# Attention in pairs of heads on the two row halves of TensorE, in one written-out order

## The chip, the cores and the metric

The kernel runs on one core of a Trainium2 chip. The metric is the device time of one execution in microseconds (us). Three executions of the kernel before took 1080.45 to 1080.77 us, median 1080.64 us.

In the text PE is TensorE (matrix products), DVE is VectorE, ACT is ScalarE, POOL is GpSimd and SP is SyncE, which here issues most of the transfers. Each engine runs its own instructions strictly one after the other; they meet only through semaphores.

## The reference

A small decoder of two layers on x of 512 tokens by 1024 features, in float32. Layer 0 mixes tokens with a gated linear recurrence, layer 1 with attention over the 128 keys of each query that an indexer scores highest; a squared-ReLU MLP follows each. The part that the change is about, shortened:

```python
q, c, qi, ki, wi = split(h @ w_in)             # 16 heads x 64, latent 128, indexer 8 heads x 64
c = rms_norm(c, kv_norm_g)                     # (512, 128): keys and values come from c
q_lat = einsum('bshd,hdc->bshc', q, w_uk) * ATT_SCALE
dots = relu(einsum('bqhd,bsd->bqhs', qi, ki))  # 8 indexer heads, 64 rows deep
score = einsum('bqh,bqhs->bqs', wi, dots)      # causal, else -inf
_, idx = top_k(score, 128)
logits = einsum('bqhc,bqkc->bqhk', q_lat, c[idx]) + rel_bias[bucket(dist)]
p = softmax(logits)                            # per head, over the chosen keys
o = einsum('bqhk,bqkc->bqhc', p, c[idx]); o = einsum('bshc,hcv->bshv', o, w_uv)
x = x + o @ w_o
x = x + square(relu(norm(x) @ w_up)) @ w_down  # the MLP, twice in the program
out = rms_norm(x, final_norm_g)                # only at the very end
```

## The kernel before

**Numbers in two halves.** A value v is kept as a high part (v rounded to fp32r) and a low part (v minus the high part); a product is three PE matmuls: high by high, low by high, high by low. ACT makes the high part with a cast (`wh`, `kh`, `pth`), DVE or POOL the low part with a subtraction (`wl`, `kl`, `ptl`).

**Weights.** The program is a sequence of weight units of 128 x 1024 (`PLAN`, `SEQ`). `prep` loads a unit over SP into `raw`, ACT casts it to `wh`, DVE subtracts to `wl`; for the units named in `LO_DMA` ACT writes -raw and a POOL transfer adds the weight on top. `unit(u)` prepares the units up to `LA = WH - 1` ahead; WH is 6, so six pairs `wh`, `wl` exist. One unit of eight 128 x 128 blocks feeds 24 matmuls of 512 columns.

**Phases.** Recurrence, MLP of layer 0, attention, w_o, MLP of layer 1, output norm. The MLP's down product is a Strassen scheme in quarters (`prod`); its last eight units (`sd1`) accumulate rows of two token tiles (`t` = 0, 1), unit by unit, each unit both tiles. Then `row` forms the two last row tiles, `rstd` their norm and `store` writes them.

**Attention.** `a_idx` multiplies out the indexer's q and k. `idx_head(h)` then takes one indexer head: its q is stacked, high part in 64 of the 128 rows and low part in the other 64 (`stack`, four half-height instructions per two heads), and so is k (`kih`, `kil`), which gives for each of the query tiles t = 1, 2, 3 (256, 384, 512 keys) two full-height matmuls into `ix`. ACT applies the ReLU, DVE (five times of 24 POOL) adds it to `score[t]`. The top 128 are found by 16 rounds of 8 for each tile (`topk_round`: `MAX8`, then `MATCH_REPLACE8` on DVE; both tiles of a round are interleaved); `topk_mask` makes a 0/-1e38 mask. Tile 1 and tiles 2 and 3 in turn are done first, then the rest of 2 and 3.

Meanwhile PE forms q for two heads per unit (`ev_q`: DVE scales, ACT and POOL stack the halves), k per head (`k_head`: three 512-column matmuls on weights that hold the head twice) and values (`v_group`). For a head, `qk` forms the logits of four query tiles by two matmuls each and adds the mask by a bf16 matmul with the identity; `qk_t` adds the bias and finds the row maximum (DVE), `qk_e` takes exponentials (ACT), `norm_p` divides (POOL), `tr` transposes on PE, `tr_ev` splits the result (ACT, DVE), `pv_head` multiplies by the values and `pv_ev` splits the output.

**What sets the order.** A scheduler sorts the whole program's instructions by the order in which they are written and by when it expects operands and buffers. Attention is written as a string `ATT_HEAD` and then a loop over heads in which `ATT_LOOP` gives the order of the steps of heads i, i-2, i-4 and i-5.

Of the kernel before, what the change touches and what calls it, by code (L numbers as in the profile page):

```python
# [33 lines left out]
WH = 6  # L34
NB = 58
NWARM = 10
SCORE_POOL = {(1, 4), (1, 5), (1, 6), (2, 6), (2, 7)}
V_DVE = {(0, 1), (0, 2)}

ATT_HEAD = ("q M p3 q q F p1 p1 q L3 q L1 L2 p1 q p2 p2 L0 p2 p1 k0 k1 p2 p1 p1 q A1 A0 v00 v"
            "01 p1 v02 n0 k2 n1 v03 q p2 p1 p1000")

ATT_LOOP = "KAa0Bk1b2xyzeGnfgm"
V_ITER = 6
WO_ITER = 4
BL = 2
TL = 2
VL = 1  # L50
# [46 lines left out]
def build_plan():  # L97
# [19 lines left out]
    for l in range(2):  # L117
        if l == 1:
# [3 lines left out]
            add("uk", [("uk", [(0, j) for j in range(g * 8, g * 8 + 8)]) for g in range(2)])  # L122
            add("a_q", lin_units("w_att", range(8), range(A_Q, A_Q + 8), 0))
            add("uv", [("uv", [(0, j) for j in range(8)])])
            add("w_o", lin_units("w_o", range(8), range(8), 3))
# [26 lines left out]
LO_DMA = {PLAN[n][0] + i for n, w in (("a_idx", range(5)), ("a_c", (0,)), ("a_q", range(8)), ("uv", (0,))) for i in w}  # L152

# [3 lines left out]
def tile_trunk(ctx: ExitStack, tc: tile.TileContext, xT, wu, prm, bias, out):  # L157
# [51 lines left out]
    state = {"next": 0}  # L209
# [26 lines left out]
    def prep(u):  # L236
# [3 lines left out]
        if UK0 <= u < UK0 + 2:  # L240
# [25 lines left out]
        for c in ((slice(0, S), slice(S, 2 * S)) if u == 0 else (slice(0, 2 * S),)):  # L266
# [4 lines left out]
            if u not in LO_DMA:  # L271
                nc.vector.tensor_sub(wl[:, c], raw[:, c], wh[:, c])  # L272
# [4 lines left out]
    def prep_to(n):  # L277
        while state["next"] < min(n, NU):
            prep(state["next"])
# [10 lines left out]
    def unit(u):  # L290
        n = u + 1 + LA
# [92 lines left out]
    def rsqrt_tok(m, w=4):  # L384
        s = st(w, "sq")
        nc.scalar.sqrt(s, m)
        y = st(w, "y")
# [7 lines left out]
    def diag(y, act=False):  # L395
# [3 lines left out]
        nc.vector.tensor_sub(dl, y, yh)  # L399
        idb = ident.unsqueeze(1).to_broadcast([P, 4, P])  # L400
        res = []
        for v in (y, dl):
            dg = bt(F32R, "dg")
            if act:
                for t in range(4):
                    nc.scalar.activation(dg[:, t * P:(t + 1) * P], ident, AF.Identity, scale=v[:, t:t + 1])
                res.append(dg)
                continue
# [5 lines left out]
    def bcast(dg, name):  # L414
        ps = pt("bc")
        nc.tensor.matmul(ps, lhsT=ones_r, rhs=dg[0], start=True, stop=False)
        nc.tensor.matmul(ps, lhsT=ones_r, rhs=dg[1], start=False, stop=True)
        b = bt(F32, name)
# [285 lines left out]
    def mlp(l, nin, up_hooks, finish):  # L704
# [31 lines left out]
        def prod(name, hooks=None):  # L736

            u, units = PLAN[name]
            for i, (kind, (_, j)) in enumerate(units):
# [666 lines left out]
```

## Time and profile before

| | |
|---|---|
| Median of three executions | 1080.64 us |
| Profiled execution, its own time | 1078.22 us |
| Its span, first to last instruction | 1076.4 us |
| PE busy | 1053.7 us, 98% |
| DVE busy | 758.0 us, 70% |
| ACT busy | 632.4 us, 59% |
| POOL busy | 141.0 us, 13% |
| Mean granted PE clock | 0.997 of full |

The rows that follow come from the profiled execution, so a time of day in them counts from the start of its span. A PE record is longer than the place it takes in the stream: consecutive matmuls overlap, and what one costs is the distance to the start of the next (below: its pitch). Attention runs from about 520 us (first `ix` product) to 692.5 us (first `w_o` product).

### The profile page before, as it was taken

The page shows a single profiled execution, that of the slowest core. Times are in us where ns is not written, and L with a number is a line of the kernel's source. Part 1 is how long each engine was busy: PE and PEld are TensorE (multiplying, and loading weights), DVE is VectorE, ACT ScalarE, POOL GpSimd, SP SyncE. Part 2 cuts the span into 40 slices and gives each one's busy share as a digit, 9 for nine tenths or more (in the row PEclk, how much of TensorE's full clock was granted, in tenths as well). Part 3 has the DMA queues.
Part 4 walks back from the last instruction along what each step waited for, and adds up shares of the span by engine and source line. Part 5 has one row for each costly group of instructions (what it writes and reads, how often), then busy time and mean ns, then how long its engine had stood idle before and what let it go on. Part 6 is the DMA issues. An engine that isn't in the chain of part 4 may idle for free.

```text
span 1076.4 us, 13486 instructions
## 1 busy us (share of the span) xinstructions
PE 1053.7 (98%) x4852; PEld 867.1 (81%) x4852; DVE 758.0 (70%) x1183; ACT 632.4 (59%) x1056; POOL 141.0 (13%) x202
## 2 busy tenths in 40 slices
PE   9999999999999999999999799999999999999996
PEld 6778888888888888888787588888888888888885
DVE  8879984555555469975799979655554544568995
ACT  7589554454544456768855898544544444456473
POOL 0000031000000000006355664221000000000000
PEclk9999999999999999999999999999999999999999
DMA  8322242444444445579662411023344344444552
GB/s 292 141 78 69 89 157 98 154 140 142 135 135 137 140 144 186 181 210 274 137 155 81 143 54 40 1 98 118 106 133 144 128 155 137 157 137 152 178 199 79
DMA packets 42691, 146.16 MB, mean 136 GB/s; under 512 B 4864, under 2 KB 4864, under 8 KB 42624
## 3 DMA queue, kind: packets, MB, share of 16 engines
q1 hardware_dynamic: 40032, 136.86, 38.5%
q0 software_dynamic: 2160, 7.87, 4.0%
q8 instruction: 38, 0.62, 0.2%
q10 hardware_dynamic: 432, 0.58, 0.2%
q14 instruction: 29, 0.24, 0.1%
HBM read 143.18 MB, written 2.10 MB: 135 GB/s over the span
## 4 chain that ended last, share of the span: by engine, by line
PE 83%; DVE 8%; ACT 5%; issue 2%; POOL 1%; DMA 0%; DVEq 0%; ACTq 0%; POOLq 0%
PE mm L298 15%; PE mm L299 15%; PE mm L300 15%; PE sp L753 9%; PE sp L751 9%; PE sp L752 9%; PE o L1168 3%; DVE work L933 2%; DVE m L928 2%; PE tr L1143 1%; DVE wl L272 1%; ACT wh L270 1%; PE qk L1097 1%; PE qk L1096 1%; PE qk L1099 1%
## 5 line engine op out<-in xcount | busy, mean ns | idle before, releaser
L270 ACT CAST wh<-raw 128x1024 fp32r<-128x1024 f32 (+1 forms) x228 | 237.6, 1049 | 345.7 <-PE mm L299 217.1
L272 DVE TENSOR_TENSOR wl<-raw,wh 128x1024 fp32r<-128x1024 f32 (+1 forms) x213 | 259.3, 1222 | 209.9 <-ACT wh L270 209.4
L298 PE MATMUL mm<-xh,wh 128*128 128x512 f32 x752 | 293.0, 390 | 0.4 <-ACT xh L358 0.4
L299 PE MATMUL mm<-xl,wh 128*128 128x512 f32 x752 | 292.9, 390 | 0.0
L300 PE MATMUL mm<-xh,wl 128*128 128x512 f32 x752 | 292.8, 389 | 0.0
L299 PEld LDWEIGHTS mm<-xl,wh 128*128 128x128 f32 x752 | 141.2, 188 | 30.3 <-DVE xl L360 1.0
L298 PEld LDWEIGHTS mm<-xh,wh 128*128 128x128 f32 x752 | 141.1, 188 | 29.7 <-ACT xh L358 0.9
L300 PEld LDWEIGHTS mm<-xh,wl 128*128 128x128 f32 x752 | 141.2, 188 | 29.3
L751 PE MATMUL sp<-wh,ah 128*128 128x512 f32 x320 | 124.9, 391 | 0.0
L753 PE MATMUL sp<-wh,al 128*128 128x512 f32 x320 | 124.6, 389 | 0.0
L752 PE MATMUL sp<-wl,ah 128*128 128x512 f32 x320 | 124.5, 389 | 0.0
L751 PEld LDWEIGHTS sp<-wh,ah 128*128 128x128 f32 x320 | 60.1, 188 | 12.7 <-ACT t L714 0.5
L753 PEld LDWEIGHTS sp<-wh,al 128*128 128x128 f32 x320 | 60.1, 188 | 12.6
L752 PEld LDWEIGHTS sp<-wl,ah 128*128 128x128 f32 x320 | 60.1, 188 | 12.2
L371 POOL TENSOR_TENSOR sq<-sq,sq 128x512 f32<-128x512 f32 x21 | 33.0, 1571 | 198.9 <-ACT sq L367 173.9
L269 POOL DMA_DIRECT2D wl<-in_wu_dram x15 | 13.2, 880 | 335.1 <-ACT wl L268 326.9
L233 DVE TENSOR_TENSOR al<-h,ah 128x512 fp32r<-128x512 f32 x80 | 54.1, 685 | 1.5 <-ACT ah L231 1.4
L751 PE MATMUL sp<-wh,sh 128*128 128x512 f32 x128 | 50.1, 391 | 0.0
L752 PE MATMUL sp<-wl,sh 128*128 128x512 f32 x128 | 49.8, 389 | 0.0
L753 PE MATMUL sp<-wh,sl 128*128 128x512 f32 x128 | 49.8, 392 | 0.0
L716 ACT ACTIVATE h<-t 128x256 f32<-128x256 f32 x128 | 46.5, 410 | 2.1
L231 ACT CAST ah<-h 128x512 fp32r<-128x512 f32 x80 | 46.6, 617 | 0.5
(258 smaller groups left out, 1634.4 us busy)
## 6 DMA issues: line engine op xcount, KB each, us to landing
raw<-in_wu_dram SPq DMA_DIRECT2D x244, 512.0 KB, 3.4
wl<-in_wu_dram POOLq DMA_DIRECT2D x15, 512.0 KB, 8.0
bias<-in_bias_dram SPq DMA_DIRECT2D x16, 256.0 KB, 3.1
x<-in_xT_dram SPq DMA_DIRECT2D x8, 256.0 KB, 6.3
out_dram<-out SPq DMA_DIRECT2D x6, 256.0 KB, 2.1
raw<-in_wu_dram SPq DMA_DIRECT2D x2, 256.0 KB, 3.6
gB<-in_prm_dram SPq DMA_DIRECT2D x2, 256.0 KB, 5.4
out_dram<-out ACTq DMA_DIRECT2D x2, 256.0 KB, 2.7
```

The costliest lines, as they stand in the source:

```text
L231: nc.scalar.copy(h, src)
L233: nc.vector.tensor_sub(l, src, h)
L270: nc.scalar.copy(wh[:, c], raw[:, c])
L272: nc.vector.tensor_sub(wl[:, c], raw[:, c], wh[:, c])
L298: nc.tensor.matmul(ps, lhsT=wh, rhs=xh, start=first, stop=False)
L299: nc.tensor.matmul(ps, lhsT=wh, rhs=xl, start=False, stop=False)
L300: nc.tensor.matmul(ps, lhsT=wl, rhs=xh, start=False, stop=last)
L371: nc.gpsimd.tensor_add(self.acc, self.acc, sq)
L716: nc.scalar.square(hq[r][half][:, p * HS:(p + 1) * HS], t[:, half * HS:(half + 1) * HS])
L751: nc.tensor.matmul(ps, lhsT=ah[:, c], rhs=wh[:, n], start=first, stop=False)
L752: nc.tensor.matmul(ps, lhsT=ah[:, c], rhs=wl[:, n], start=False, stop=False)
L753: nc.tensor.matmul(ps, lhsT=al[:, c], rhs=wh[:, n], start=False, stop=last)
```

## The change

Seven edits.

1. **Row halves.** Two heads now lie one in rows 0 to 63 and one in rows 64 to 127, and each product of 64 rows is issued twice in a row, once on each half of the array (`rows3`, `tile_position`). A pair of heads takes 3 x 2 half-height matmuls where it took 2 x 2 full-height ones with stacked parts. q and k are split with full-height instructions, `stack` is gone. The k weights hold two heads beside each other: 8 `k_head`, `k_hi`, `k_lo` in place of 16, and one `uk` unit in place of two.
2. **Index scores.** ReLU is applied in PSUM for tiles 2 and 3 and DVE reads it there; tile 1 (all eight heads) goes to POOL.
3. **Engines.** Scaling q moves from DVE to ACT and POOL, all value low parts to POOL, the mask's multiplication from ACT to POOL.
4. **Top-k.** Tile 1 goes with tile 3 for eight rounds and then with tile 2 for eight, then 2 and 3.
5. **Order.** The string `ATT` of 530 steps, each of one engine, is issued word for word by `tc.manual_schedule()`. Weight units are prepared by steps `W`; the low parts of the first four `w_o` units are separate steps `Y`. Two of the eight q units come later (`a_r`).
6. **Buffers.** WH 6 to 5 (lookahead of four units, none inside `ATT`), NB 58 to 62.
7. **End.** The last three units of `sd1` are held and run token tile by token tile. The final norm of a row tile has fewer steps (`rstd1`).

```diff
-WH = 6
-NB = 58
+WH = 5
+NB = 62
...
-ATT_HEAD = ("q M p3 q q F p1 p1 q L3 q L1 L2 p1 q p2 p2 L0 p2 p1 k0 k1 p2 p1 p1 q A1 A0 v00 v"
...
-ATT_LOOP = "KAa0Bk1b2xyzeGnfgm"
...
+NQ = 6
+ATT = (
+    "M0.0 M1.0 q.0 M2.0 p.0 q.1 p.1 W.4 M3.0 M4.0 L.0 p.2 q.2 p.3 u1.1 u2.1 p.4 F0.0 p.5 p.6 F1.0 p.7 q.3 W.5  "
...
+    def rows3(pss, w, lts, rts, last):
+        for n, (lt, rt) in enumerate(((lts[0], rts[0]), (lts[1], rts[0]), (lts[0], rts[1]))):
+            for e in range(2):
+                nc.tensor.matmul(pss[e], lhsT=lt[HR[e]], rhs=rt[HR[e], :w], start=(n == 0), stop=(last and n == 2),
+                                 tile_position=(64 * e, 0))
...
+    def idx_pair(j):
+        q = qi.pop(j)
         for t in (1, 2, 3):
             w = (t + 1) * P
...
+            pss = [pt("ix")[:, :w] for _ in range(2)]
+            rows3(pss, w, [a[:, t * P:(t + 1) * P] for a in q], (kih, kil), True)
+            for e in range(2):
+                if t == 1:
...
+                    nc.gpsimd.tensor_add(score[t][:, :w], score[t][:, :w], rl)
+                    continue
+                nc.scalar.activation(pss[e], pss[e], AF.Relu)
...
-            topk_round((1, 3 - i % 2))
+            topk_round((1, 3 if i < TOPK // 16 else 2))
...
-        if qs:
-            nc.vector.tensor_mul(qf, ps, ab["r8"])
...
+    def q_scale(i):
+        nc.gpsimd.tensor_mul(qf[i], qf[i], ab["r8"])
...
-    def qk(h, part):
-        q = qs[h // 2][h % 2]
-        kh, kl = kst[h]
...
+        for t in PARTS[part]:
             w = (t + 1) * P
             n = max(256, w)
...
+            rows3(pss, n, [a[:, t * P:(t + 1) * P] for a in qs[p]], k, t == 0)
+            for h, pst in zip(heads, pss):
+                if t:
...
+                    nc.tensor.matmul(pst, lhsT=identb, rhs=mask[t][:, :n], start=False, stop=True)
...
+    with tc.manual_schedule():
+        for w in ATT.split():
+            k, i = w.split(".")
...
             for i, (kind, (_, j)) in enumerate(units):
                 w = unit(u + i)
-                wh, wl, ah, al = w if len(w) == 4 else w + aop[j].pop(kind)
+                held.append((j, w if len(w) == 4 else w + aop[j].pop(kind)))
...
+                if len(units) - 4 < i < len(units) - 1 and name == "sd1":
+                    continue
                 for t in range(2):
-                    for p in range(2):
+                    for (j, (wh, wl, ah, al)), p in ((g, p) for g in held for p in range(2)):
...
+        def rstd1(i):
+            s = st(1, "fs")
+            nc.scalar.activation(s, ss[:, i, 0:1], AF.Sqrt, scale=1.0 / D, bias=me[0][:, i:i + 1])
...
```

Of `ATT`, the letters that the text uses: q forms q, V values, K keys, p is one step of the top-k, y a mask, A, B and C are the logits of a pair for tiles 0 and 1, 2, 3, T transposes, G multiplies by the values.

PE, first index scores. Before: `qia` and `qib` are the stacked q of two heads, `kih` and `kil` k's two parts, one row a full-height matmul:

```order
L864 MATMUL ix_4414<-kih_4192,qia_4280 128x256
L865 MATMUL ix_4414<-kil_4193,qia_4280 128x256
L864 MATMUL ix_4420<-kih_4192,qia_4280 128x384
L865 MATMUL ix_4420<-kil_4193,qia_4280 128x384
L864 MATMUL ix_4426<-kih_4192,qia_4280 128x512
L865 MATMUL ix_4426<-kil_4193,qia_4280 128x512
L864 MATMUL ix_4432<-kih_4192,qib_4281 128x256
```

The same place now; `qih` and `qil` are the parts of two heads, and of two rows that differ only in the `ix` number the first works in rows 0 to 63 and the second in rows 64 to 127:

```order
L897 MATMUL ix_4398<-kih_4185,qih_4270 128x256
L897 MATMUL ix_4399<-kih_4185,qih_4270 128x256
L897 MATMUL ix_4398<-kih_4185,qil_4272 128x256
L897 MATMUL ix_4399<-kih_4185,qil_4272 128x256
L897 MATMUL ix_4398<-kil_4186,qih_4270 128x256
L897 MATMUL ix_4399<-kil_4186,qih_4270 128x256
L897 MATMUL ix_4414<-kih_4185,qih_4270 128x384
L897 MATMUL ix_4415<-kih_4185,qih_4270 128x384
```

Two heads took four matmuls per width, and now take six of half height, in three twins.

PE, logits of tiles 2 and 3 in the loop over heads. Before, one head (`qb`, its keys `kh` and `kl`), with the masks:

```order
L1096 MATMUL qk_5469<-kh_5282,qb_4797 128x384
L1097 MATMUL qk_5469<-kl_5284,qb_4797 128x384
L1099 LDWEIGHTS identb
L1099 MATMUL qk_5469<-mask_4211,identb 128x384
L1096 MATMUL qk_5474<-kh_5282,qb_4797 128x512
L1097 MATMUL qk_5474<-kl_5284,qb_4797 128x512
L1099 LDWEIGHTS identb
L1099 MATMUL qk_5474<-mask_4212,identb 128x512
```

Now tile 3 of a pair of heads (two `qk` numbers), one of the 24 such blocks in the loop:

```order
L897 MATMUL qk_5376<-kh_5267,qh_5179 128x512
L897 MATMUL qk_5377<-kh_5267,qh_5179 128x512
L897 MATMUL qk_5376<-kh_5267,ql_5188 128x512
L897 MATMUL qk_5377<-kh_5267,ql_5188 128x512
L897 MATMUL qk_5376<-kl_5274,qh_5179 128x512
L897 MATMUL qk_5377<-kl_5274,qh_5179 128x512
L1177 LDWEIGHTS identb
L1177 MATMUL qk_5376<-mask_4205,identb 128x512
L1177 LDWEIGHTS identb
L1177 MATMUL qk_5377<-mask_4205,identb 128x512
```

The mask matmuls stay full height and follow the twins directly, so the array goes from half height to full height and back at each block.

DVE, late in the top-k (tiles 2 and 3). Before, `qf` (scaled q) and `kl` stand between the searches:

```order
L928 MAX m_692_5069<-work_4614 128x8
L928 MAX m_693_5071<-work_4607 128x8
L1015 TENSOR_TENSOR qf_4984<-mm_4959,rB_545_4357 128x512
L933 MATCH_REPLACE work_4614<-m_692_5069,work_4614 128x384
L933 MATCH_REPLACE work_4607<-m_693_5071,work_4607 128x512
L928 MAX m_694_5075<-work_4614 128x8
L928 MAX m_695_5077<-work_4607 128x8
L1070 TENSOR_TENSOR kl_5045<-k_5039,kh_5043 128x512
```

Now at the same place:

```order
L964 MAX m_654_5000<-work_4817 128x8
L964 MAX m_655_5002<-work_4600 128x8
L969 MATCH_REPLACE work_4817<-m_654_5000,work_4817 128x384
L969 MATCH_REPLACE work_4600<-m_655_5002,work_4600 128x512
L964 MAX m_660_5033<-work_4817 128x8
L964 MAX m_661_5035<-work_4600 128x8
L969 MATCH_REPLACE work_4817<-m_660_5033,work_4817 128x384
L969 MATCH_REPLACE work_4600<-m_661_5035,work_4600 128x512
```

The searches follow each other; the other DVE work of attention stands behind them.

## Rows read from the trace of the kernel before

**Rows 1.** The page, part 1: busy time, share of the span, instructions.

```profile
PE 1053.7 (98%) x4852; PEld 867.1 (81%) x4852; DVE 758.0 (70%) x1183; ACT 632.4 (59%) x1056; POOL 141.0 (13%) x202
```

**Rows 2.** Stages: window, length, busy PE, PEld, DVE, ACT, POOL, clock, DMA.

```profile
520.63:540.90 20.27, 19.66 (x99) 16.70 (x98) 16.10 (x28) 14.92 (x32) 8.35 (x10) 1.00 0.44 112
540.90:580.00 39.10, 39.10 (x178) 32.45 (x178) 39.07 (x123) 22.88 (x37) 23.32 (x22) 1.00 0.63 149
580.00:616.01 36.01, 27.84 (x135) 20.86 (x134) 35.97 (x100) 25.97 (x62) 22.00 (x29) 0.95 0.30 98
616.01:652.74 36.73, 36.53 (x230) 30.66 (x229) 30.12 (x93) 33.24 (x90) 22.65 (x49) 1.00 0.20 64
652.74:669.40 16.66, 16.66 (x109) 14.18 (x109) 15.70 (x50) 14.89 (x44) 8.09 (x22) 1.00 0.11 32
```

**Rows 3.** What PE waited for, 560 to 620: us, times, longest.

```profile
PE qk L1096 <- ACT kh L1068: 4.6, 3, 2.0
PE qk L1096 <- DVE stat L1112: 2.2, 1, 2.2
```

**Rows 4.** PE in order of time, value products (o) of one head.

```profile
685.54 0.48 PE L1168 MATMUL o<-pth,vh 128*128 128x512 f32 x1
685.86 0.40 PE L1168 MATMUL o<-ptl,vh 128*128 128x512 f32 x1
686.09 0.40 PE L1168 MATMUL o<-pth,vl 128*128 128x512 f32 x1
...
686.33 0.34 PE L1168 MATMUL o<-pth,vh 128*128 128x384 f32 x1
686.51 0.34 PE L1168 MATMUL o<-ptl,vh 128*128 128x384 f32 x1
...
686.86 0.28 PE L1168 MATMUL o<-pth,vh 128*128 128x256 f32 x1
686.98 0.28 PE L1168 MATMUL o<-ptl,vh 128*128 128x256 f32 x1
```

**Rows 5.** Chain that ended last, 684 to 688: start, us, what.

```profile
684.70 1.09 PE tr L1143 x10
```

**Rows 6.** DVE busy in the searches (MAX8, MATCH_REPLACE8), q scaling, masks.

```profile
540.31:599.20 58.89, 24.52 (x48) 0.97 0.43 102
...
540.31:599.20 58.89, 27.33 (x96) 0.97 0.43 102
...
L1015 DVE TENSOR_TENSOR qf<-mm,rB 128x512 f32<-128x512 f32 x6 | 4.0, 665 | 0.0
...
L938 DVE TENSOR_TENSOR work<-work,score x3: 403/541/671, 574.3 to 598.5; 128x256 f32<-128x256 f32 x1, 128x384 f32<-128x384 f32 x1, 128x512 f32<-128x512 f32 x1
```

**Rows 7.** POOL in order of time: one head of index scores, tile 1.

```profile
534.31 0.78 POOL L869 TENSOR_SCALAR rl<-rl,wt 128x256 f32<-128x256 f32 x1
535.17 1.05 POOL L871 TENSOR_TENSOR score<-score,rl 128x256 f32<-128x256 f32 x1
```

**Rows 8.** End of the program, DVE and ACT in order of time.

```profile
1067.55 0.75 DVE L784 SCALAR_TENSOR_TENSOR o<-sp,r,vx 128x512 f32<-128x512 f32 x1 [0.61 <-PE sp L753]
...
1071.48 0.75 DVE L1278 SCALAR_TENSOR_TENSOR out<-o,y,gB 128x512 f32<-128x512 f32 x1
...
1068.34 0.63 ACT L1267 ACTIVATE sq<-o 128x512 f32<-128x512 f32 x1 [0.57 <-DVE o L784]
1068.87 0.19 ACT L1267 ACTIVATION_READ_ACCUMULATOR sq<-o 128x1 f32 x1
1068.96 0.18 ACT L386 ACTIVATE sq<-mf 128x1 f32<-128x1 f32 x1
...
1069.18 0.16 DVE L388 RECIPROCAL y<-sq 128x1 f32<-128x1 f32 x1 [0.63 <-ACT sq L386]
1069.38 0.16 DVE L390 TENSOR_TENSOR t<-y 128x1 f32<-128x1 f32 x1
```

**Rows 9.** Stage window in the last product of the second MLP.

```profile
999.00:1026.00 27.00, 27.00 (x121) 22.36 (x120) 26.43 (x33) 12.91 (x17) 0.00 (x0) 1.00 0.53 176
```

More of the change, by code (lines that the diff above doesn't have):

```diff
@@ L149 @@
 NMEM = len(MEM)
-LO_DMA = {PLAN[n][0] + i for n, w in (("a_idx", range(5)), ("a_c", (0,)), ("a_q", range(8)), ("uv", (0,))) for i in w}
+LO_DMA = {PLAN[n][0] + i for n in ("a_idx", "a_c", "a_q", "uv", "a_r") for i in range(len(PLAN[n][1]))}
 @with_exitstack
@@ L234, in split_act, with prep @@
         return h, l
-    def prep(u):
+    def prep(u, late=None):
         raws = pre_raw.pop(u) if u in pre_raw else load_raw(u)
@@ L271, in prep @@
             if u not in LO_DMA:
-                nc.vector.tensor_sub(wl[:, c], raw[:, c], wh[:, c])
+                if late is not None:
+                    late[u] = lambda: nc.vector.tensor_sub(wl, raw, wh)
+                else:
+                    nc.vector.tensor_sub(wl[:, c], raw[:, c], wh[:, c])
         prepped[u] = (wh, wl)
@@ L275, in prep, with prep_to @@
             prepped[u] += split_act(aq.pop((kind, SEQ[u][1][1])), "a")
-    def prep_to(n):
+    def prep_to(n, late=None):
         while state["next"] < min(n, NU):
-            prep(state["next"])
+            prep(state["next"], late)
             state["next"] += 1
@@ L412, in diag, with diag_act, bcast_mm @@
         return res
-    def bcast(dg, name):
+    def diag_act(v):
+        dg = bt(F32R, "dg")
+        for t in range(4):
+            nc.scalar.activation(dg[:, t * P:(t + 1) * P], ident, AF.Identity, scale=v[:, t:t + 1])
+        return dg
+    def bcast_mm(dg):
         ps = pt("bc")
@@ L934, in topk_round, with need @@
                                     imm_value=NEG_SCORE)
+    did = set()
+    def need(*steps):
+        assert did.issuperset(steps), steps
     def topk_mask(t):
@@ L1108, in qk_t @@
         rs, nm, _ = stat[h]
-        todo, b = todos[h, part]
-        for t, w, pst in todo:
+        did.add(("t", h, part))
+        b = bts[h]
+        for t, w, pst in todos[h, part]:
             bs = b[:, (3 - t) * P:(3 - t) * P + w]
@@ L1139, in tr @@
         lay = LAY[i]
+        need(("n", h, 1))
+        if i != 1:
+            need(("n", h, 0))
         ps = pt("tr")
@@ L1227, in tile_trunk, with pv_hi @@
-    for i in range(2, NH + BL + TL + VL):
-        if i + 2 < NH:
-            load_bias(i + 2)
-        if V_ITER <= i < V_ITER + 4:
-            v_group(1, i - V_ITER)
-        if i == WO_ITER:
-            prep_to(WO0 + LA)
-        for a in ATT_LOOP:
-            d, fn = ACTS[a]
-            if 0 <= i + d < NH and not (i + d < 2 and a in "Aaen") and not (i + d < 3 and a in "Kk"):
-                fn(i + d)
+    def pv_hi(h):
+        if h // 2 not in os_:
+            os_[h // 2] = [bt(F32R, "oh"), None]
+        r = slice((h % 2) * 64, (h % 2) * 64 + 64)
+        nc.scalar.copy(os_[h // 2][0][r], ops[h][r])
```

405 lines of the change are left out of this document (211 added, 194 removed), and 23 rows, old and new, of the table ATT.

## Prediction

> **What bounds the kernel now.** Read the busy shares first: PE is busy for 98% of the span [rows 1]. Microseconds come from giving PE less to do or from the stretch where it stands still. The stage windows come second, and they show where that stretch is [rows 2]. In 540.90 to 580.00 PE is full and DVE is full beside it (39.07 of 39.10). In 580.00 to 616.01 PE is busy for 27.84 of 36.01 us, DVE for 35.97. From 616 on PE is full again and DVE has room (30.12 of 36.73, 15.70 of 16.66). So one stage of attention, the end of the top-k, is bound by DVE, and the rest by PE. The view of PE's waits names what it stood for [rows 3]: the cast of k on ACT, 4.6 us in three waits, and a DVE result, 2.2 us in one. Neither is slow work; both wait because what precedes them on DVE is the search or is queued behind it. The granted clock there is 0.95 [rows 2]: with the two levels 1 and 0.5 that is 3.6 us at half speed, during the standstill.
>
> Third comes the price of a PE matmul, its pitch [rows 4]: 512 columns 0.23 us (685.86 to 686.09), 384 columns 0.18, 256 columns 0.12. A transpose of 128 columns costs 0.11 (ten in 1.09 us) [rows 5].
>
> **The change part by part.** The sum is made against the profiled execution (1078.22 us, span 1076.4, so 1.8 us lie around it). It is 2.42 us shorter than the median 1080.64; I subtract the gain from the median.
>
> *Keys.* 8 in place of 16 `k_head` remove 8 x 3 matmuls of 512 columns: 24 x 0.23 = 5.5 us of PE, in a stage where PE is on the path or will be. Certain by the code.
>
> *Index scores and logits on row halves.* The trace before has no half-height matmul, so a twin (the same product on both halves) is bounded from both sides. If the halves work at the same time, a twin costs the pitch of one matmul; if one after the other, two. Index: before 8 heads x 2 x (0.12+0.18+0.23) = 8.5 us; side by side 4 pairs x 3 x 0.53 = 6.4, gain 2.1; in turn 12.7, loss 4.2. Logits without masks (the masks stay): before 16 x 2 x (0.12+0.12+0.18+0.23 = 0.65) = 20.8; side by side 8 x 3 x 0.65 = 15.6, gain 5.2; in turn 31.2, loss 10.4. I take side by side: the rows of each twin read other rows of SBUF and write another PSUM bank, so nothing that a matmul of the trace occupies is asked for twice, except perhaps the weight load (a rival below).
>
> *Changes between half and full height.* By the order rows there are 26 blocks of twins (24 of logits, 2 of index scores), 52 changes. None is in the trace. Lower bound 0; upper bound the part of a record that lies behind its pitch, 0.40 - 0.23 = 0.17 us, if the array must empty: 8.8 us. The nearest row is the change from transposes to value products: 685.54 to 685.86 is 0.32, that is 0.09 over the pitch [rows 4]. 52 x 0.09 = 4.7 us lost. The Trainium skill, "TensorEngine Tiling (Array Packing)", Key Properties, speaks against the change here: it says that going to another tiling mode empties TensorE. By that rule the upper bound would hold, the sum below would be 4.1 us worse, 1067.3; no run here shows it yet.
>
> *The standstill.* DVE's searches take 24.52 + 27.33 us of records for 48 + 96 instructions [rows 6]; back to back they overlap by some 0.07 each for the 96 long ones and the value loads hide no more, so about 48 us, of the 58.9 from the first search to the last mask comparison at 598.5. The other 10 us are q scaling (six of 0.66 in the window), k and value low parts, small steps and mask work [rows 6]. The new order leaves about 3 us of that between the searches (the order rows). The start: it needs tile 1's score, now a POOL chain of 0.78 + 1.05 = 1.83 us per head [rows 7], the last four heads from their first product on, 7.3 us. The first block of index scores is 1.0 us shorter, so this ends about 1.7 us before the old start (540.3), at 538.6; with 48 + 1.4 of comparisons + 3 the last mask is there at about 591, eight us earlier. PE meanwhile: index blocks and one wait are about 3 us shorter, so its q stage starts at 537.9 in place of 540.9, and before the first logits that need mask 2 stand 8 units x 24 x 0.23 = 44.2, six value groups and four keys (10 x 0.69 = 6.9) and about 2 of small products and first logits: 591.0. The two meet. So the standstill goes: 36.01 - 27.84 = 8.2 us of idle, half of the 3.6 us at half clock = 1.8, and 0.17 for each of the four waits shown, in which a record hides its own tail, 0.7: together 10.7. What is late next is the loop behind it. Per pair of heads PE now needs 11.1 (two thirds of 16.66 us for three heads [rows 2]) less 0.69 for k and 0.65 for the logits: 9.8 us; DVE's records 10.5 less one `kl` of 0.69, also 9.8, though they overlap a little; ACT 9.9 less 0.6. The engines stand closer than before, when this loop lost 0.2 us in 36.7. I charge 3.0 us of new PE idle over eight pairs and the meeting point. None of it comes at nothing: q scaling goes to ACT and POOL, which have room there (25.97 and 22.00 of 36.01), and POOL's mask multiplications precede PE's need by under a microsecond.
>
> *End.* The last three units now finish tile 0 18 matmuls (4.1 us) before the end, so its norm is done beside PE. For tile 1 the old path from the last product to the last `store` is 1067.55 to 1071.48, 3.9 us, with the two chains in each other's way. The new one by the same rows: to the square 0.79, square and read 0.72, root to reciprocal 0.22, three small steps of 0.20: 2.3 [rows 8]. Gain 1.6.
>
> *Buffers.* One unit less of lookahead is at most 24 x 0.23 = 5.5 us of lead, in the down products 2.8. PE waits nowhere for weights outside the first microseconds, so I take 0. Cover is thinnest where DVE is full, 26.43 of 27 us [rows 9]; if it goes there, up to 2.8 us. Moving two q units, the `uk` unit and the DMAs costs PE nothing: transfers use 0.30 of the queues' time there [rows 2], and the same units are loaded less one.
>
> *Sum.* 5.5 + 2.1 + 5.2 + 10.7 + 1.6 = 25.1; less 4.7 and 3.0: 17.4. 1080.64 - 17.4 = 1063.2, forecast 1063.
>
> **Rivals.** (a) *The halves work in turn.* The slower side, one mechanism: twins cost two pitches. Instead of gaining 7.3 the twins lose 14.6, so 1063.2 + 21.9 = 1085.1, slower by 4.5 us, with the changes of height still paid. It decides from the point where a twin costs more than about 1.8 pitches (17.4 of 21.9). For it: no row shows two matmuls at once. Against: as above.
>
> (b) *Weight loads are the bound of a twin.* Each half needs its own load; where a stream is short the load sets the pace, as in the transposes, 0.11 each for 128 columns [rows 5], so a twin takes at least 0.22. Logits per pair 3 x (0.22+0.22+0.22+0.23) = 2.7 in place of 1.95, eight times: +5.8; index +1.7. 1070.7. For it: the transposes. Against: 256 columns run at 0.12 with a load each, so loads of 0.11 are nearly hidden already.
>
> The Trainium skill, "TensorE: Matmul & The Clock Gate", Measured speedup vs the span model, gives 3.07 for four row tiles side by side at 512 columns. Read as 0.77 of the ideal, an estimate: a twin would cost 1.3 pitches and the time would be 1063.2 + 0.3 x 22.0 = 1069.8. No run here shows it yet.
>
> (c) *A fixed order waits where a scheduler would not.* DVE or ACT become the bound of the loop: 10% over PE's 9.8 us in seven pairs is 6.9 us, 1070. For it: the equal loads above, and that an instruction which waits holds up all behind it on its engine (a `p` step behind a late score, a transpose split behind a late exponential). Against: the loop before was dense at 94% of DVE (15.70 of 16.66).
>
> (d) *Everything fits.* No price for changes of height and no new idle: 1055.5.
>
> (e) *It does not do what it says:* the standstill stays as long as it was, 1063.2 + 10.7 - 3.0 = 1070.9, should the first score or mask be late by what the searches gain.
>
> **How the numbers follow.** Forecast 45%, its own range 1059 to 1067; (d) 14%; (b) 14%; (c) and (e) together 15%; (a) 9%, and 3% for something near no change. Between 1055 and 1074 lie the forecast, most of (d), (b), (c) and (e): 8 in 10. What one can tell from no change is 0.2%, 2.2 us; slower beyond that only with (a), 9%; same 3%; faster 88%.
>
> **What the new profile would show.** Twins whose starts lie a few hundredths apart while the next twin follows a pitch later mean side by side; starts 0.23 apart for 512 columns mean (a), 0.11 apart throughout mean (b). The matmul behind each twin block shows the price of a change. The window from the first search to the third mask should shrink from 59 to about 52 us and PE's idle before the first masked logits be under 1 us; a granted clock of 1 there confirms it. Waits of PE for DVE or ACT of more than 3 us in the loop mean (c). From the last product to the last store 2.3 us. I would be wrong above all through the twins: their 22 us of PE are the largest unseen number.

## The result and the profile after

The changed kernel took 1061.06 to 1061.59 us in four runs, median 1061.33; the kernel before 1080.08 to 1080.77 in its four, median 1080.55. The ratio is 0.9823, 95% interval 0.9806 to 0.984: 19.2 us less, and the forecast was 1063. The profiled execution of after took 1061.24 us, its span is 1059.3. Spans are compared below, and they differ by 17.1 us, since the profiled execution of before was a short one (in later runs the kernel before took anything from 1077.99 to 1080.86 us). Against 17.1 the forecast's 17.4 has to be held. Where the 2 us between the two differences lie, the two traces cannot show.

The page of after, part 1, answers to [rows 1]; columns are busy time, share of the span and instructions:

```profile
PE 1045.8 (99%) x4910; PEld 857.6 (81%) x4916; DVE 743.2 (70%) x1141; ACT 621.2 (59%) x1038; POOL 138.7 (13%) x210
```

PE is the bound more than ever. Six of its 4916 records are missing from this trace. To see where the time went, both spans are cut at the same four events: first index product, end of the second index block, first `w_o` product, last product. First the kernel before, then after (window, length, busy PE, PEld, DVE, ACT, POOL, clock, DMA):

```profile
520.63:535.49 14.86, 14.24 (x76) 12.22 (x74) 11.33 (x22) 12.23 (x28) 3.17 (x5) 1.00 0.50 118
535.49:692.54 157.05, 148.69 (x827) 123.28 (x826) 144.46 (x416) 116.92 (x278) 89.40 (x149) 0.99 0.30 81
692.54:1067.12 374.58, 374.58 (x1673) 310.19 (x1672) 231.82 (x264) 184.10 (x284) 11.35 (x7) 1.00 0.41 135
1067.12:1076.38 9.26, 0.39 (x2) 0.00 (x0) 3.74 (x15) 2.99 (x8) 0.00 (x0) 0.80 0.30 113
```

```profile
518.74:535.28 16.54, 15.28 (x98) 11.00 (x97) 9.29 (x18) 12.25 (x28) 8.48 (x14) 1.00 0.76 223
535.28:677.28 142.00, 140.29 (x861) 114.43 (x867) 127.40 (x378) 108.35 (x264) 84.74 (x151) 1.00 0.28 75
677.28:1051.87 374.59, 374.59 (x1674) 310.39 (x1672) 237.68 (x276) 186.72 (x288) 11.42 (x7) 1.00 0.43 139
1051.87:1059.33 7.46, 0.39 (x2) 0.00 (x0) 2.20 (x6) 1.74 (x4) 0.00 (x0) 0.72 0.36 141
```

| stage | before | after | difference | forecast |
|---|---|---|---|---|
| start to first index product | 520.63 | 518.74 | -1.9 | 0 |
| index products | 14.86 | 16.54 | +1.7 | -1.7 (2.1 gained, 0.4 for changes of height) |
| to the first `w_o` product | 157.05 | 142.00 | -15.05 | -14.1 (5.5 + 5.2 + 10.7 less 4.3 and 3.0) |
| to the last product | 374.58 | 374.59 | 0 | 0 |
| to the end | 9.26 | 7.46 | -1.8 | -1.6 |
| sum | | | -17.1 | -17.4 |

The large stage came out within 1 us of its forecast, as a sum; two of its terms were off by about 3 us each, in opposite directions (last section but two). Index products went the wrong way, and 1.9 us that no term foresaw made up for half of that.

Twins in the loop, PE in order of time (start, duration, line, matmul; x2 is two of them together):

```profile
639.33 0.39 PE L1177 MATMUL qk<-mask,identb 128*128 128x256 bf16 x2
639.66 0.50 PE L897 MATMUL qk<-kh,qh 64*128 64x512 f32 x2
639.99 0.40 PE L897 MATMUL qk<-kh,ql 64*128 64x512 f32 x2
640.22 0.40 PE L897 MATMUL qk<-kl,qh 64*128 64x512 f32 x2
640.55 0.61 PE L1177 MATMUL qk<-mask,identb 128*128 128x512 bf16 x2
```

From the second twin to the third is 639.99 to 640.22, 0.23 us: a twin of 512 columns costs the pitch of one matmul [rows 4]. The price of the change of height stands in three places: the two masks of 256 columns take 0.33 where twice 0.12 would do (+0.09), the first twin 0.33 in place of 0.23 (+0.10), the last twin again 0.33 (+0.10). The 24 blocks of logits show this, 0.27 to 0.35 us each, where nothing else waits and no record is missing.

The window in which PE stood still before [rows 2], and PE's waits from the last index block to `w_o` (us, times, longest), to be held against [rows 3]:

```profile
580.00:616.00 36.00, 35.45 (x225) 25.89 (x227) 32.46 (x106) 32.92 (x84) 30.64 (x47) 1.00 0.14 45
```

```profile
PE qk L1177 <- issue: 0.8, 5, 0.2
PE st L397 <- ACT csq L1014: 0.7, 1, 0.7
```

PE is busy for 35.45 of 36 us where it was for 27.84, the clock is 1.00 in place of 0.95, and no wait for DVE or for k is left. The five of 0.2 us are no waits: each stands where one of the missing records, a mask product of 512 columns (0.23 us), belongs; in the trace of the kernel with paired masks (below) no record is missing, and it shows none of them. Masks of tiles 2 and 3 on POOL, and the first products that use them on PE:

```profile
592.72 0.83 POOL L985 TENSOR_SCALAR mask<-work 128x384 bf16<-128x384 f32 x1
...
594.25 0.62 POOL L985 TENSOR_SCALAR mask<-work 128x512 bf16<-128x512 f32 x1
```

```profile
595.62 0.50 PE L1177 MATMUL qk<-mask,identb 128*128 128x384 bf16 x2
...
596.95 0.39 PE L1177 MATMUL qk<-mask,identb 128*128 128x512 bf16 x1
```

Both masks are there 2.1 us before they are needed (592.72 + 0.83 = 593.55 against 595.62).

The end, DVE, which answers to [rows 8]:

```profile
1052.30 0.75 DVE L817 SCALAR_TENSOR_TENSOR o<-sp,r,vx 128x512 f32<-128x512 f32 x1 [0.81 <-PE sp L785]
...
1054.81 0.75 DVE L1360 SCALAR_TENSOR_TENSOR out<-o,fy,gB 128x512 f32<-128x512 f32 x1
```

From the last row tile to its output step 2.51 us (2.3 forecast), 3.93 before. Another 0.4 us is behind it, probably because only one row tile's stores are under way at the end, not two; no run separates that.

### The profile page after: what moved, and what is told of

It is laid out like the page before. It is cut to its first block, busy times and chain, and to the rows that moved or that the text cites. A ratio compares the mean times of both kernels' runs of the same rounds, so it can differ in the third digit from the quotient of the medians.

```text
span 1059.3 us, 13463 instructions
## 1 busy us (share of the span) xinstructions
PE 1045.8 (99%) x4910; PEld 857.6 (81%) x4916; DVE 743.2 (70%) x1141; ACT 621.2 (59%) x1038; POOL 138.7 (13%) x210
## 4 chain that ended last, share of the span: by engine, by line
PE 96%; ACT 2%; DVE 1%; issue 0%; DMA 0%; DVEq 0%; ACTq 0%
PE mm L315 19%; PE mm L316 18%; PE mm L317 18%; PE sp L783 10%; PE sp L785 10%; PE sp L784 10%; PE o L1265 3%; PE qk L897 2%; PE tr L1235 2%; PE qk L1177 1%; PE gt L315 1%; PE gt L316 1%; PE gt L317 0%; ACT wh L284 0%; PE st L397 0%
## 5 line engine op out<-in xcount | busy, mean ns | idle before, releaser
L289 DVE TENSOR_TENSOR wl<-raw,wh 128x1024 fp32r<-128x1024 f32 (+1 forms) x209 | 253.5, 1219 | 172.8 <-ACT wh L284 171.0
L268 DVE TENSOR_TENSOR raw<-raw,raw 128x1024 f32<-128x1024 f32 x16 | 19.6, 1225 | 54.9 <-DMA raw<-in_wu_dram 54.9
```

## The experiments

The theory: twins run side by side, the standstill went because DVE was freed for the search, the end is shorter by the held units and the shorter norm. Rivals: half-height products are cheap by themselves; the standstill went for another reason; and for the misses, what holds PE in the index blocks and what brought the early 1.9 us. Times are held against after's 1061.33 us. After was not run again beside them; a kernel that differs from it in nothing that costs (three and three, below) ran beside three of them (masks between, ReLU in SBUF, q on DVE) and took 1061.07 us.

### Are the halves at work at once?

The second head's products on the first head's half, so that this kernel leaves out the second head of each pair:

```diff
-                nc.tensor.matmul(pss[e], lhsT=lt[HR[e]], rhs=rt[HR[e], :w], ..., tile_position=(64 * e, 0))
+                nc.tensor.matmul(pss[e], lhsT=lt[HR[0]], rhs=rt[HR[0], :w], ..., tile_position=(0, 0))
```

> The second head's products of index scores and logits use the first head's operands, all on rows 0 to 63, in the same order and number; the second head of each pair is thus computed from the wrong rows. What is told apart: do the halves work at once, or are half-height products as such cheap? Theory (at once): every pair now costs two pitches, 22 us more of PE, less the changes of height (the masks still change it), 1080 to 1084. Rival (the half-height product itself runs in half the time): 1061. In the trace neighbours then start 0.23 us apart for 512 columns.

Measured 1078.57 us (1078.17 to 1079.08), 17.2 more than after. A block of 512 columns on PE:

```profile
646.23 0.72 PE L897 MATMUL qk<-kh,qh 64*128 64x512 f32 x2
646.80 0.62 PE L897 MATMUL qk<-kh,ql 64*128 64x512 f32 x2
647.26 0.62 PE L897 MATMUL qk<-kl,qh 64*128 64x512 f32 x2
```

646.80 to 647.26 is 0.46, two pitches. From the last index block to `w_o` it is 157.38 us, 15.4 more than after; the logits have 8 x 3 x 0.65 = 15.6 us of pitches, so the second half is paid in full there and was free before. The index stage lost only 2.1 of 6.4: PE waits there anyway. The halves do work at once. That I expected 1080 to 1084 is the index stage again, which I still took to be full of products.

### Must the two halves stand next to each other?

```diff
-        for n, (lt, rt) in enumerate(((lts[0], rts[0]), (lts[1], rts[0]), (lts[0], rts[1]))):
-            for e in range(2):
+        for e in range(2):
+            for n, (lt, rt) in enumerate(((lts[0], rts[0]), (lts[1], rts[0]), (lts[0], rts[1]))):
```

> The same six half-height products per block, but three on rows 0 to 63 first and then three on rows 64 to 127, so that neighbours in the stream share a half. Theory (two halves run at once only when neighbouring instructions lie on different halves): a pair of heads costs 5 pitches in place of 3 per width (only the meeting point overlaps), 2/3 of the 22 us that the twins take now in index scores and logits, +14.6 us of PE; part of it in the loop may be hidden nowhere, so 1074 to 1078. Rival (the gain has nothing to do with adjacency, PE looks further ahead or half-height products are cheap by themselves): unchanged, 1061.

Measured 1061.07 us (1060.97 to 1061.39): no difference. My theory on neighbours fell. A block of 512 columns, in which the first head's three products (`kh,qh`, `kh,ql`, `kl,qh`) are issued before the second head's three:

```profile
639.31 0.51 PE L897 MATMUL qk<-kh,qh 64*128 64x512 f32 x2
639.64 0.40 PE L897 MATMUL qk<-kh,ql 64*128 64x512 f32 x2
639.88 0.41 PE L897 MATMUL qk<-kl,qh 64*128 64x512 f32 x2
```

The records still come in twins of equal operands: the fourth product of the stream starts with the first, ahead of the second and third. PE takes work for an idle half from behind waiting work of the other, so the first section's "strictly one after the other" holds for PE only within a half. How far behind, six and six show (index scores of tiles 1 and 2, logits of tiles 0 and 1):

```diff
-        for t in PARTS[part]:
-            ...
-            rows3(pss, n, ...)
+        for e in range(2):
+            for t in PARTS[part]:
+                rows3(..., es=(e,))
```

> Further apart than three and three: logits of tiles 0 and 1 as six products on one half, then six on the other; index scores of tiles 1 and 2 likewise six and six (tile 3 three and three). Three and three cost nothing. Theory (PE takes products for an idle half from far ahead in its queue): 1061 to 1061.5, second half starting within 0.05 us of the first. Rival (it looks only a few products ahead): where the reach is three to four, the last two or three of each block of twelve run alone: 8 blocks x 0.24 to 0.36 and 4 index blocks x 0.35 to 0.5, 3 to 5 us more, 1064 to 1066.

Measured 1062.53 us (1062.17 to 1062.86). One block of twelve products of 256 columns:

```profile
638.82 0.38 PE L897 MATMUL qk<-kh,qh 64*128 64x256 f32 x1
639.04 0.28 PE L897 MATMUL qk<-kh,ql 64*128 64x256 f32 x1
639.16 0.28 PE L897 MATMUL qk<-kl,qh 64*128 64x256 f32 x1
639.17 0.39 PE L897 MATMUL qk<-kh,qh 64*128 64x256 f32 x2
...
639.62 0.28 PE L897 MATMUL qk<-kh,qh 64*128 64x256 f32 x1
...
640.07 0.39 PE L1187 MATMUL qk<-mask,identb 128*128 128x256 bf16 x2
```

The second half starts at 639.17, when the third product of the first half starts and only three are left before it. Two to three products at the front and three at the back run alone: 0.35 us more per block, in eight blocks 2.8, and the stage to `w_o` is 2.5 us longer (144.50). So the reach is three to four products; seven of the eight blocks look like this one, and in the other the second half starts 0.1 us later. The total rose by 1.2 only, because the index stage got 1.3 us shorter in that order; why was not followed up.

The Trainium skill, "TensorE: Matmul & The Clock Gate", The mechanism, says that matmuls start and end strictly in program order. The two traces above do not agree: across the two row halves a later one starts first. The measurement decides.

### What does a change of height cost?

More of them, with the masks of tile 1 between the twins of tile 0 and of tile 1:

```diff
+            if t == 1:
+                need(("mask", t))
+                for pst in pss:
+                    nc.tensor.matmul(pst, lhsT=identb, rhs=mask[t][:, :n], start=True, stop=False)
-            rows3(pss, n, ..., t == 0)
+            rows3(pss, n, ..., t < 2, t != 1)
             for h, pst in zip(heads, pss):
-                if t:
+                if t > 1:
```

> In the eight blocks of tiles 0 and 1 the two mask products stand between the twins of tile 0 and those of tile 1 instead of behind both: 16 more changes of height, no other work. My forecast's price of 0.09 us each: +1.4 us, 1062.8. Price as the trace after shows it (about 0.2 from full to half height, 0.1 to 0.2 back): +2 to +2.5 us, 1063.5. If the extra in a block belongs to the start of a block and not to the height: under 0.3 us.

Measured 1063.34 us (1062.44 to 1064.02), 2.0 more, which looks like 0.13 us for each of 16 changes. The trace, of the slowest of the four executions, says otherwise on two counts. In four of the eight places the twins of tile 3 now follow those of tile 1 with no mask between, so there are only four blocks more, eight changes: 1.2 us at 0.29 a block, 0.7 at my 0.09 a change. And of the 2.8 us by which the stage to `w_o` is longer, 1.5 lie in its first 6 us, ahead of all logits, where the granted clock fell for a while to the lower of its two levels (0.75 in the mean, 1.00 in after):

```profile
535.12:541.00 5.88, 5.88 (x21) 4.75 (x21) 4.08 (x9) 1.14 (x3) 2.55 (x5) 0.75 0.76 171
```

The other 1.4 us fit the price from the rows of after, 1.2, better than mine, 0.7. How much of the 2.0 in the median is clock, the traces do not tell.

Does such a cost belong to the height, or to any change in kind? Transposes, logits and masks in the kernel before, all at full height:

```profile
626.22 0.38 PE L1143 MATMUL tr<-ident,pb 128*128 128x128 f32 x2
626.36 0.42 PE L1096 MATMUL qk<-kh,qb 128*128 128x384 f32 x1
626.62 0.34 PE L1097 MATMUL qk<-kl,qb 128*128 128x384 f32 x1
626.80 0.34 PE L1099 MATMUL qk<-mask,identb 128*128 128x384 bf16 x1
626.84 0.53 PE L1096 MATMUL qk<-kh,qb 128*128 128x512 f32 x1
627.21 0.40 PE L1097 MATMUL qk<-kl,qb 128*128 128x512 f32 x1
```

The first product behind a change is long, but it starts early by as much: 0.03 us behind the last transpose, 0.04 behind the mask. From 626.22 to 627.21 is 0.99 us, and the pitches of what stands there make 0.99 (two transposes, three products of 384 columns, one of 512). In full height such changes cost nothing; the cost of a twin block is that of the height. The Trainium skill, "TensorEngine Tiling (Array Packing)", Key Properties (another tiling mode empties the array), agrees in kind. Here it costs 0.19 us from full to half height (0.09 and 0.10) and 0.10 back, 0.145 in the mean, where I had taken 0.17 as the upper bound.

Fewer changes, on top of the next experiment's edit: masks are held back until another PE step or a reader of the block comes.

```diff
-                    nc.tensor.matmul(pst, lhsT=identb, rhs=mask[t][:, :n], start=False, stop=True)
+                    later.append((p, part, pst, t, n))
...
+            if k[0] in "MFqVKTG" or ...:
+                masks()
```

> With ReLU in SBUF (1059.45), and the masks of a block of logits held back until another PE step or a reader of the block comes: 18 changes from twins to masks in place of 24 and 5 from masks to twins in place of 11, by the order of the instructions. Theory (a change costs 0.1 at the end of the twins and 0.19 back): 6 x 0.29 = 1.7 us less, 1057.7. Rival (the later masks hold up the readers on DVE in the loop): 1059.5 or slower.

Measured 1059.00 us (1058.81 to 1059.28), 0.45 less than without, not 1.7, within the spread of the runs of the two. The stage to `w_o` fell from 142.48 to 142.15. Most of what six pairs of changes should give was lost again, above all in two of the joined blocks, which from 594.13 and 599.60 us on take some 0.8 and 0.6 us beyond their products and edges. That the later masks hold up their readers there is argued, not shown.

### What holds PE in the index blocks?

```diff
-                nc.scalar.activation(pss[e], pss[e], AF.Relu)
+                rl = bt(F32, "rl")[:, :w]
+                nc.scalar.activation(rl, pss[e], AF.Relu)
-                nc.vector.scalar_tensor_tensor(out=score[t][:, :w], in0=pss[e], ...
+                nc.vector.scalar_tensor_tensor(out=score[t][:, :w], in0=rl, ...
```

> ReLU of tiles 2 and 3 of the index scores is written to SBUF again and DVE reads it there, so that a PSUM bank comes free after ACT and not only after DVE. Theory (PE stands 3 us in the two index blocks because ix banks are held until DVE has read them): the blocks go from 5.25 and 5.62 us to about 4.3 and 4.6, the time to 1059.5. Rival (the wait is for ACT's ReLU chain, or what is won there is lost again in front of the first masked logits): blocks unchanged, or shorter with the total at 1061.

Measured 1059.45 us (1058.96 to 1060.35), 1.9 less than after. The index stage, and the one behind it:

```profile
518.66:533.14 14.48, 14.23 (x98) 10.80 (x97) 10.77 (x16) 11.26 (x25) 9.97 (x13) 1.00 0.81 230
533.14:675.62 142.48, 140.70 (x861) 114.61 (x867) 128.94 (x380) 109.28 (x268) 87.50 (x153) 1.00 0.29 76
```

16.54 became 14.48; the blocks take 4.18 and 4.63 us in place of 5.25 and 5.62. The theory stands: with ReLU written back to PSUM, a bank (the piece of PSUM that one product writes) came free for the next product only after DVE. The waits that the view named in after are these, and they show less than half of the loss, since the rest hides in stretched records:

```profile
PE ix L897 <- DVE score L915: 1.0, 4, 0.3
```

What still holds the blocks should be ACT. Tested on top of ReLU in SBUF and of the paired masks:

```diff
-                    nc.scalar.activation(rl, pss[e], AF.Relu)
-                    nc.gpsimd.tensor_scalar(out=rl, in0=rl, scalar1=wt[...], scalar2=1.0, op0=ALU.mult, op1=ALU.mult)
+                    nc.vector.tensor_scalar(out=rl, in0=pss[e], scalar1=0.0, scalar2=wt[...], op0=ALU.max, op1=ALU.mult)
```

> On top of ReLU in SBUF and paired blocks (1059.0): ReLU and weight of tile 1 in one DVE instruction from PSUM, POOL only adds. What still holds PE in the index blocks (4.18 and 4.62 us, 3.4 would be side by side with the changes of height) should be ACT, which needs 2.5 us of ReLU for a pair where PE needs 1.6. Theory: blocks 0.4 to 0.5 us shorter each, POOL's chain shorter too, 1058.1. Rival: 3 us more on DVE next to the search make the masks late by more than their 2 us of room: 1059 to 1060.

Measured 1057.43 us (1057.08 to 1057.79), ratio to before 0.979 (0.9775 to 0.9805): 3.9 us faster than after with its three edits, the fastest of all. The same two stages:

```profile
518.94:532.62 13.68, 13.44 (x97) 10.78 (x96) 12.65 (x21) 9.74 (x19) 6.19 (x7) 1.00 0.83 236
532.62:673.94 141.32, 139.79 (x863) 115.44 (x867) 128.50 (x383) 108.49 (x265) 85.06 (x150) 1.00 0.29 78
```

Blocks of 3.79 and 4.22, 0.4 shorter each, as expected. The second stage is 0.8 shorter than with the paired masks alone (142.15). There, as with ReLU in SBUF alone, the mask of tile 2 was ready just when it was needed (593.67 against 593.72; 593.54 against 593.59); here it is ready at 591.12 and needed at 593.01, and some 0.6 of the 0.8 are gained in the 4 us behind that point.

### Did the relief of DVE end the standstill?

```diff
-        nc.gpsimd.tensor_mul(qf[i], qf[i], ab["r8"])
+        nc.vector.tensor_mul(qf[i], qf[i], ab["r8"])
```

> The scaling of q goes back from POOL to DVE, in the same order of steps: six scalings of 0.66 us, 4.0 us, then stand between the searches. Theory (the standstill went because DVE was relieved; the masks of tiles 2 and 3 come 2.1 us before PE needs them in the trace after): masks 4.0 us later, PE waits 1.9 us in front of the first masked logits, the time 1063.2. Rival (DVE had room between the searches, the end of the standstill is due to the other parts): 1061.3.

Measured 1063.23 us (1062.51 to 1064.43), 1.9 more, as the theory had it. The trace bears out only a part of the way there. The mask of tile 2 on POOL, and PE:

```profile
595.25 1.48 POOL L985 TENSOR_SCALAR mask<-work 128x384 bf16<-128x384 f32 x1 [4.50 <-DVE work L980]
```

```profile
596.79 0.48 PE L1177 MATMUL qk<-mask,identb 128*128 128x384 bf16 x2 [0.40 <-POOL mask L985]
```

The mask ends at 596.73, 3.2 us later than in after; 0.7 of that is a later start of attention in this trace (first index product 519.45 against 518.74). So it is 2.5 us late, not 4.0: of the eight scalings that the edit moves, four stand between the searches and a fifth ahead of the mask. With 2.1 us of room PE should wait 0.4, and it waits 0.40. The stage to `w_o` is 1.8 us longer (143.84), and only some 0.5 of it are lost at that product. Another 1.1 are lost by 606 us; PE waits there once more, 0.4 for the statistics that DVE forms of the logits, and for the rest the view names nobody. So the relief of DVE was needed, and the room of the mask priced its own wait well, but that the total came out to the tenth is luck.

The same steps in the same order of writing, sorted by the scheduler:

```diff
-    with tc.manual_schedule():
+    with nullcontext():
```

> The changed kernel with its steps written in the same order, but sorted by the scheduler as everything else is, in place of the order word for word. Theory (the gain is row halves, fewer keys and work taken off DVE; the literal order is worth little): 1061 to 1062. Rival (the standstill only goes because the other DVE work is kept behind the searches): the scheduler puts work between the searches again, masks 2 to 8 us later than PE needs them, 1063 to 1069.

Measured 1070.85 us (1070.66 to 1070.94), 9.5 more. My theory fell, and so did the place that the rival named: the mask of tile 2 is ready at 591.72, earlier than in after. The loss is behind it. Two stretches of that kernel, PE's longest wait group from 592 to 687, and DVE at the same place:

```profile
592.81:600.00 7.19, 5.61 (x36) 3.30 (x36) 6.90 (x13) 5.01 (x11) 7.19 (x7) 1.00 0.98 330
600.00:607.00 7.00, 6.91 (x30) 3.92 (x30) 5.18 (x24) 5.91 (x22) 4.95 (x9) 0.53 0.28 101
```

```profile
PE qk L897 <- DVE stat L1191: 1.6, 2, 1.1
```

```profile
593.10 4.00 DVE L287 TENSOR_TENSOR wl<-raw,wh 128x1024 fp32r<-128x1024 f32 x2 [1.75 <-ACT wh L284]
597.02 0.28 DVE L1191 CUSTOM_DVE_ANT_0 pa<-qk,bias 128x128 f32<-128x128 f32 x1
```

The first logits are done at 593.7, but DVE reads them only at 597.02: the scheduler put weight low parts in front, four of them between 590.1 and 599.4, which the written order has as the steps `Y` from 647 us on. PE waits for the PSUM that DVE reads, stands for 1.6 of 7.2 us, and then the granted clock is at 0.53 for seven, almost all of it at the lower of its two levels: at most 3.3 us lost there, and 3.9 us of waits up to `w_o`. The remainder of the 9.5 was not taken apart.

### The end

Two kernels with one execution each, so only their traces are used. First the last three units unit by unit again:

```diff
-                if len(units) - 4 < i < len(units) - 1 and name == "sd1":
-                    continue
```

> The last three units again unit by unit, each for both token tiles; the shorter norm stays. From the last product's start to the end of the span it is 9.26 us before and 7.46 after. If the hold is what helps (tile 0's norm and stores done beside PE): the two tiles' rows are 1.36 us apart again, their steps share DVE and ACT and their stores the queues, 0.6 to 1.2 us longer, 8.1 to 8.7. If the shorter norm is what helps: 7.5.

From the last product to the end 9.29 us: without the held units the shorter norm is worth nothing. The reason is on DVE:

```profile
1053.24 0.75 DVE L1358 SCALAR_TENSOR_TENSOR out<-o,fy,gB 128x512 f32<-128x512 f32 x1
1053.91 0.74 DVE L815 SCALAR_TENSOR_TENSOR o<-sp,r,vx 128x512 f32<-128x512 f32 x1
```

Tile 1's row (L815) starts only behind tile 0's output step, although its product had ended near 1052. The new code writes norm and output of tile 0 ahead of tile 1's row; that is right with held units and wrong without, so the two edits belong together and this run does not split them cleanly. Then the old norm with the held units:

```diff
-            y = rstd1(i)
+            y = rstd((i,))
```

> The old norm of a row tile (sum, scale, root, then three small steps) with the held units. Theory: of the 1.8 us about 0.5 are the norm's fewer steps (two small DVE instructions of 0.2 each ahead of the root), so 7.9 from the last product's start to the end. If the norm were the whole gain: 9.2.

7.90 us: the shorter norm is worth 0.44, as expected, and the held units with their order the other 1.4.

### The early 1.9 us

```diff
-WH = 6
+WH = 5
```

> The kernel before with one pair of weight buffers less, nothing else. In the trace after, the work ahead of attention ends 1.9 us earlier (first index product 518.74 against 520.63), which no term of my sum holds; in the two traces PE waits less for DVE's diagonal of the norm (bc products) there. Theory (fewer weight low parts stand ahead of the norm's steps on DVE, because the lookahead is shorter): first index product near 518.7, and 1078 to 1079 in all if attention gives nothing back. Rival 1 (it comes from other parts of the change, the order of the scheduler for one): 520.6 and 1080. Rival 2 (my fear for the shorter lookahead): weights late in the down products, up to 2.8 us more, 1082.

On the kernel before: 1078.41 us (1077.78 to 1079.38), ratio 0.9989 (0.998 to 0.9998). First index product at 519.92 in place of 520.63. The median of ten runs is 1.1 us under that of the kernel before in the same series (1079.55), so the shorter lookahead helps a little by itself. In the trace about 0.7 of the 1.9 us come with it, at the first norm, where the second broadcast product no longer waits 0.75 us for DVE (0.68 behind the first, 2.98 before). The other 1.2 us to 518.74 lie for the most part at the norm ahead of attention; their cause is open. In the eleven other kernels made from after, whose code is the same up to there, the first index product came at 518.12 to 519.45, so a single trace knows this only to about 0.7 us, and the split is rough.

## Why the prediction was right, step by step

- *Bound by PE, 98%.* Right; now 99%.
- *Keys, 5.5, and logits, 5.2.* Right. By the instructions of the stage and the pitches of [rows 4, 5], the products from the last index block to `w_o` fell by 10.7 us. The twins, the largest unseen number, cost one pitch, and the same-half run priced the other case: rival (a) would have given 1078.6, not 1085.1, for the most part because the index stage waits anyway (4.3 us of the difference). Rival (b) and the estimate of 1.3 pitches from the Trainium skill ("TensorE: Matmul & The Clock Gate", Measured speedup vs the span model) are out: 0.23 us for a twin of 512 columns, 0.12 for 256.
- *Changes of height, 4.7.* Mis-sized, and its row was misread. That a change costs something was right; measured are 0.19 and 0.10 us, 0.29 a block, so the 24 blocks of logits alone make 7.0 us where the forecast had 4.3 for them. The row that it took for the price, 0.32 in place of 0.23 behind the transposes [rows 4], is no price: as at 626.36 above, that product starts 0.08 us early, 0.03 behind the last transpose, and over both the change costs nothing. It came near the size by luck.
- *Standstill, 10.7, and new idle, 3.0.* The standstill went, as forecast. The search ran from 538.2 to the last mask comparison in 55.0 us, against 52 forecast and 58.9 before, and PE's first masked logits came at 593. That it began near the forecast 538.6 is luck: attention itself began 1.9 us early, and from the first index product to the first search it is 19.4 us, 19.7 before and 18.0 forecast. Apart from its products the stage fell by 4.4 us (15.05 less 10.7), with 7.0 of new changes of height in it, so standstill and new idle together brought 11.4, not 7.7: the shown waits of 8.3 us went to 0.7 (in front of the latent's norm), the 1.8 us at the lower clock level came back, and the new idle of 3.0 hardly came. The rest hides in stretched records. With the scaling of q on DVE 1.9 us are lost again, and only some 0.5 of them at the mask. How much each part of the relief gave, no run shows. Rival (e) is out. So is rival (c): it said that a fixed order waits where a scheduler would not, and it was the scheduler that waited, 9.5 us.
- *Index scores, 2.1.* This step failed. I counted products and took PE to be the bound in the two blocks. Side by side PE is so fast there that the banks decide, which ACT and then DVE must empty: the stage grew by 1.7. I wrote that ReLU moves into PSUM and that DVE reads it there, and did not ask how long a bank is then held. ReLU into SBUF turned 16.54 into 14.48, and a lighter ACT into 13.68; the forecast was 13.2.
- *End, 1.6.* Right in size (1.8). The working held: 2.51 us for the last row against 2.3; the 0.4 behind the last output step I had not counted.
- *Buffers, 0.* Right from `w_o` on: 374.58 and 374.59. Ahead of attention the shorter lookahead even helped, by about 0.7 us in one trace and 1.1 in the median of ten runs.

The sum was close partly by luck. 3.4 us too many were forecast as gain in the index stage, and 1.9 us at the start and 1.0 in the large stage went the other way; inside the large stage 2.7 us more for changes of height met 3.7 us more from the standstill and the idle that did not come. Of rival (d) one half came true, no new idle; the other, no price for the changes of height, did not.

## What to carry to other kernels

Two products of half height on the two row halves cost one pitch, and each block of them 0.3 us at its edges. Before you price such an edge from a single long pitch, look at the start before it too: a product that starts early by as much costs nothing. When PE gets faster in a stage, ask at once who empties its PSUM banks and when each is released: an elementwise step that writes back to PSUM holds the bank for the next reader too. The slack of a mask, read from two rows of the trace, told to the tenth how long PE would wait for that mask, but not what the same work costs further on: that was several times as much. And look at the clock of a stretch before you price an edit from its length.

## What the runs showed of the hardware

- The order in the stream need not alternate between the halves: three and three cost nothing, six and six lose 0.35 us per block of twelve; PE starts products for an idle half from three to four places further back, ahead of earlier ones.
- A change costs 0.09 us on the last product ahead of it and 0.10 on the first behind it, from full to half height; from half height to the bf16 masks 0.10 in all. In full height alone a change from transposes to products or from bf16 masks to logits costs nothing: the first product behind it is 0.09 or 0.14 longer in pitch and starts early by as much.
- After 1.6 us of standing in 7.2, the longest wait 1.1, PE ran at 0.53 of its clock for seven microseconds (almost all at the lower of its two levels, 1.2 GHz). In after no wait in attention was over 0.7 us, and the clock stayed at 1.00; but in one execution of a kernel whose index blocks are the same it fell to the lower level at their end and cost 1.5 us behind them.
- The mean granted clock was 0.998 or 0.999 in the executions of after and of the kernels made from it, but 0.995 to 0.996 under the scheduler and 0.997 in the two single ones; for the kernel before it was 0.992 to 0.997.
